# Smaller blocks in the recurrent stage of a hybrid decoder layer: 64-row diagonal blocks, 32x32 completions, alternating row halves, broadcasts by transposes

## The chip, the core and the metric

One of the cores of a Trainium2 chip runs the whole layer. The time is that of the device in microseconds (us), from one launch. TensorE is called PE here (its weight loads PEld), VectorE DVE, ScalarE ACT, GpSimd POOL, SyncE SP. All data are float32.

## The reference: what is computed

One decoder layer on 2048 tokens of width 1024. A root-mean-square norm and one input projection feed three branches, and one output projection adds them to the residual: differential attention (4 heads, two softmax maps each), a gated short convolution, and RWKV-7 time mixing. The change lies almost wholly in the last:

```
def step(state, inp):                  # per head, state is 64 x 64
    r_t, k_t, v_t, w_t, kk_t, a_t = inp
    sa = einsum('bhvk,bhk->bhv', state, kk_t)
    state = state * w_t - sa * (kk_t * a_t) + v_t * k_t
    y = einsum('bhvk,bhk->bhv', state, r_t)
```

It has 4 heads of 64. The output goes through a group norm per head and a gate.

## The kernel before

**Stages.** The kernel runs normalization and the first projections, then the recurrence of the first 1024 tokens (`rwkv(0)`), the attention of these tokens, the recurrence of the other 1024, their attention, and the output projection. Beside the recurrences and the attentions runs a *filler* stream: the remaining input projections (L343: 24 matmuls of 128x128 by 128x512 for one result) and at the end the output projection (L1194).

**The recurrence.** The steps are solved in chunks of 64 tokens. A *unit* is 256 tokens (4 chunks) of two heads, one head on partitions 0 to 63, the other on 64 to 127; a half has 8 units, the kernel 16. A unit goes through:

- `early`: decays, scaled keys, norms. The reciprocal norm of a token is broadcast over partitions by a matmul with the identity (`bc`, L538).
- `scores`: the products `G` of keys and queries inside the chunks (L572): per head 4 matmuls that contract over the 64 rows of that head, with 128 weight columns and 128 moving columns. DVE masks them into `N`, `BB` and `DE`. `N` is held as 128x128 matrices, of which only the two 64x64 diagonal blocks are not zero. The 32x32 diagonal blocks of `N` go through memory into another layout, `U`.
- `inverse`: DVE solves the 32x32 triangles (L638 to L649), and the inverses go through memory into the diagonal 32x32 blocks of `Z` (L653, L658).
- `late`: completes the 64x64 inverses. `Z` is transposed by PE (`xp`, L673, four 128x128), copied out by ACT, multiplied by `N` (`p4`, L680), masked and copied by ACT (L682), multiplied by `Z` (`p5`, L685), and added into `Z` by DVE (L688). Then `wu` (L696) applies the inverse, `mr` (L717, L718, 16 matmuls for each parity `e` of a chunk) makes the transition matrices `M` and `RW`, and four steps carry the state through the chunks: `chp` (L738), a copy of the state by DVE (L740), `yp` (L743). Group norm and gate follow, with a broadcast by matmul (`bcp`, L765).

**Order of the work.** PE runs strictly in the order in which the program issues its matmuls. The generators of the recurrence and the attention give a hint at every `yield` (in us); `run` multiplies it by a factor (0.6 and 0.55 for the two recurrences) and issues that much filler from the stream before it goes on. Between two pieces of `late(n)` lies one piece of the unit two ahead (`chain(n+2)`: `early`, `scores`, `inverse`). The order on the other engines is set by a planner when the program is built; each engine then runs its queue in order. DMAs are issued by SP. `ps_s` has three PSUM banks, which `xp`, `wu`, `mr`, `G` and `tp` take in turn; `ps_j` has two for the filler.

Outside the recurrence, `spread` (L251) broadcasts the input norm and `finish` in the attention (L1060) the norm of the result, both by matmuls with the identity. `hs`, `sr`, `nr` in the code are slices of 64 partitions.

Of the kernel before, what the change touches and what calls it, by code (L numbers as in the profile page):

```python
# [87 lines left out]
def _table(cols):  # L88
    t, o = {}, 0
    for n, w in cols:  # L90
# [7 lines left out]
                      ("eye", 32 * GW), ("hmean", 2), ("id64", 64), ("mB", 2)))  # L98
# [4 lines left out]
def host_consts():  # L103
# [21 lines left out]
    q = p % 64  # L125
    put("mB", np.stack([q >= 32, q < 32], 1))
# [19 lines left out]
def trunk(ctx, tc, a, o, phases="RTO"):  # L146
# [65 lines left out]
    # row blocks of the gated mix, transposed: heads by 256 tokens, conv and rwkv by 512  # L212
# [35 lines left out]
    def spread(rs, ps=None):  # L248
        ps = pj("hbc") if ps is None else ps
        for j in range(4):  # L250
            mm(ps[:, j * P:(j + 1) * P], rs[:, j:j + 1].broadcast_to([P, P]), ident, start=True, stop=True)  # L251
        bc = ap.tile([P, CK], F32, name="ccs", bufs=2)
        cpy(bc, ps)
        return bc
# [11 lines left out]
    def stats0(c, xs, pool, raw):  # L266
        """1/rms of the tokens, broadcast; with raw, the products with the unscaled input come first."""
# [40 lines left out]
    # ------------------------------------------------------------------ input projection  # L308
# [145 lines left out]
    # ------------------------------------------------------------------ rwkv  # L454
    def rwkv(half, pool):
# [15 lines left out]
        for i in range(2):  # L471
            m = {}
            for n, w in (("N", P), ("Z", P)):
                m[n] = pool.tile([P, NQ, w], F32, name=f"{n}{i}")
                nc.gpsimd.memset(m[n], 0.0)
            mats.append(m)
        P1 = pool.tile([P, NQ, P], F32, name="P1")
        nc.gpsimd.memset(P1, 0.0)
        mB = C("mB")
# [7 lines left out]
        def early(s, n, g, ct):  # L487
# [49 lines left out]
            for j in range(NJ):  # L537
                mm(bcp[:, j * P:(j + 1) * P], rnb[:, 2 * j:2 * j + 2].rearrange("p a b -> p (a b)"), ident,  # L538
                   start=True, stop=True)
# [9 lines left out]
        def scores(s):  # L549
# [17 lines left out]
            for jj in range(NJ // 2):  # L567
                for h in range(2):
                    G = pS("G")
                    for q in range(4):  # L570
                        j, e = jj * 2 + q // 2, q % 2
                        mm(G[:, q * P:(q + 1) * P], KB[h * 64:h * 64 + 64, j, 2 * e:2 * e + 2],  # L572
                           RA[h * 64:h * 64 + 64, :, j, 1 - e], start=True, stop=True)
                    Gv = G.rearrange("p (j e m t) -> p j e m t", j=2, e=2, m=2)
                    q0 = h * NJ + jj * 2
                    for e in range(2):
# [3 lines left out]
                        tt(N[sr, q0:q0 + 2, sr], Gv[sr, :, e, 1], lt[sr], ALU.mult)  # L580
# [7 lines left out]
            for e in range(2):  # L588
                for b in range(2):
                    q0 = (e * 2 + b) * NQ  # L590
                    r0 = 64 - 64 * e + b * 32
                    dma(ud[q0:q0 + NQ].rearrange("q s t -> s q t"), N[r0:r0 + 32, :, r0:r0 + 32])
# [39 lines left out]
        def inverse(s):  # L632
            U, Z = s["U"], s["Z"]
            # inverses of the 32x32 diagonal blocks by forward substitution, GW columns of one block per partition;
            # the odd rows are first freed of the even rows before them, so that two rows go at a time
# [18 lines left out]
            for e in range(2):  # L654
                for b in range(2):
                    q0 = (e * 2 + b) * NQ
                    r0 = 64 - 64 * e + b * 32
                    dma(Z[r0:r0 + 32, :, r0:r0 + 32], zd[q0:q0 + NQ].rearrange("q c i -> c q i"))  # L658

        def late(s):  # L660
# [4 lines left out]
            Z2 = Z.rearrange("p q (b n) -> p q b n", b=2)  # L665
            Pb2 = P1.rearrange("p q (b n) -> p q b n", b=2)
# [3 lines left out]
            X = T("X", (P, NQ, 64))  # L670
            xp = pS("xp")
            for q in range(NQ):
                nc.tensor.transpose(xp[:, q * P:(q + 1) * P], Z[:, q], ident)  # L673
            yield LQ[0]
            cpy(X.rearrange("p q (b n) -> p (q b) n", b=2), xp.rearrange("p (q n) -> p q n", n=64)[:, :, 0:32])
            yield LQ[0]
            p45 = pw("p45")
            p4, p5 = p45[:, 0:NQ * 64], p45[:, NQ * 64:2 * NQ * 64]
            for q in range(NQ):
                mm(p4[:, q * 64:(q + 1) * 64], N[:, q], X[:, q], start=True, stop=True)  # L680
            yield LQ[0]
            act(Pb2[:, :, :, 0:32], p4.rearrange("p (q b n) -> p q b n", q=NQ, b=2), AF.Copy, scale=mB[:, 0:1])  # L682
            yield LQ[0]
            for q in range(NQ):
                mm(p5[:, q * 64:(q + 1) * 64], P1[:, q], Z2[:, q, :, 32:64], start=True, stop=True)  # L685
            yield LQ[0]
            Z64 = Z.rearrange("p q (b n) -> p (q b) n", b=2)
            stt(Z64[:, :, 32:64], p5.rearrange("p (q n) -> p q n", n=32), mB[:, 1:2], Z64[:, :, 32:64], ALU.mult,  # L688
                ALU.add)
            yield LQ[0]  # L690
            # [W | U0]
            W = T("W", (P, NQ, 64))
            wu = pS("wu")
            for h in range(2):
                for j in range(NJ):
                    mm(wu[:, (h * NJ + j) * P:(h * NJ + j + 1) * P], Z[:, h * NJ + j], AB[:, j, h], start=True, stop=True)  # L696
# [6 lines left out]
            for r0 in (0, 64):  # L703
                nc.gpsimd.memset(Z[r0:r0 + 32, :, r0 + 32:r0 + 64], 0.0)
            dP4 = dP.rearrange("p (j e) n -> p j e n", e=2)
            yield LQ[1]
            # transition matrices and the read-out of the incoming state
# [671 lines left out]
```

## Time and profile before

| | us |
|---|---|
| median of 3 runs | 1854.19 |
| lowest, highest | 1853.9, 1865.09 |
| span of the profiled execution | 1855.8 |

| engine | busy us | share of the span |
|---|---|---|
| PE | 1723.0 | 93% |
| PEld | 1288.3 | 69% |
| DVE | 1228.7 | 66% |
| POOL | 817.9 | 44% |
| ACT | 737.5 | 40% |

The span is the profiled execution's own time, and durations come from it; it lies 0.1% above the median of the runs. Busy time is the union of an engine's instructions. A matmul's own duration holds its way through the array, so that the time one takes from the engine is read from start to start. A float32 matmul stands in the trace as two records, a transpose as one.

### The profile page before, as it was taken

The page shows a single profiled execution, that of the slowest core. Times are in us where ns is not written, and L with a number is a line of the kernel's source. Part 1 is how long each engine was busy: PE and PEld are TensorE (multiplying, and loading weights), DVE is VectorE, ACT ScalarE, POOL GpSimd, SP SyncE. Part 2 cuts the span into 40 slices and gives each one's busy share as a digit, 9 for nine tenths or more (in the row PEclk, how much of TensorE's full clock was granted, in tenths as well). Part 3 has the DMA queues.
Part 4 walks back from the last instruction along what each step waited for, and adds up shares of the span by engine and source line. Part 5 has one row for each costly group of instructions (what it writes and reads, how often), then busy time and mean ns, then how long its engine had stood idle before and what let it go on. Part 6 is the DMA issues. An engine that isn't in the chain of part 4 may idle for free.

```text
span 1855.8 us, 27286 instructions
## 1 busy us (share of the span) xinstructions
PE 1723.0 (93%) x9416; PEld 1288.3 (69%) x9416; DVE 1228.7 (66%) x2653; ACT 737.5 (40%) x1797; POOL 817.9 (44%) x786
## 2 busy tenths in 40 slices
PE   5899799999999889999799999999999989999998
PEld 4687576777776666777666767766666666767686
DVE  7534866656527888756766576357788888777742
ACT  5331111221126555532122221145565656666642
POOL 6443332333286776334222233473485473453233
PEclk8899898998999999999799998999999989999999
DMA  5342121222156442124222222351142243232223
GB/s 181 114 146 93 47 63 59 86 76 67 61 181 196 148 140 82 64 68 148 63 82 68 86 76 62 100 154 60 63 147 64 74 150 101 71 95 70 81 78 116
DMA packets 136586, 180.13 MB, mean 97 GB/s; under 512 B 34912, under 2 KB 83072, under 8 KB 136448
## 3 DMA queue, kind: packets, MB, share of 16 engines
q1 hardware_dynamic: 136448, 178.39, 30.8%
q8 instruction: 74, 1.21, 0.3%
q14 instruction: 64, 0.52, 0.1%
HBM read 132.18 MB, written 46.14 MB: 96 GB/s over the span
## 4 chain that ended last, share of the span: by engine, by line
PE 62%; DVE 25%; DMA 4%; issue 3%; SPq 2%; ACT 2%; POOL 1%; DVEq 0%; POOLq 0%; ACTq 0%
PE pj L343 27%; PE ops L1194 9%; PE S L938 6%; DVE tmpx L646 5%; PE aT L1021 3%; PE S L937 3%; DVE Xs L649 3%; PE G L572 2%; PE av L1012 2%; DVE P L986 2%; SPq L594 2%; PE av L1014 2%; PE av L1013 2%; DVE x L242 1%; DVE nm L943 1%
## 5 line engine op out<-in xcount | busy, mean ns | idle before, releaser
L343 PE MATMUL pj<-hh,wh 128*128 128x512 f32 x1008 | 424.4, 421 | 4.2 <-DVE raw L394 3.4
L343 PE MATMUL pj<-hl,wh 128*128 128x512 f32 x1008 | 423.8, 420 | 0.0
L343 PE MATMUL pj<-hh,wl 128*128 128x512 f32 x1008 | 423.2, 420 | 0.0
L946 ACT ACTIVATE P<-S,nm 128x512 f32<-128x512 f32 (+3 forms) x320 | 199.3, 623 | 162.9 <-DVE nm L943 143.6
L943 DVE TENSOR_REDUCE nm<-S 128x1 f32<-128x512 f32 (+3 forms) x320 | 192.5, 606 | 77.4 <-PE S L938 74.1
L329 POOL TENSOR_TENSOR wl<-wr,wh 128x1024 fp32r<-128x1024 f32 x85 | 209.6, 2465 | 46.8 <-ACT wh L324 41.2
L343 PEld LDWEIGHTS pj<-hh,wh 128*128 128x128 f32 x1008 | 195.9, 194 | 49.1 <-issue 7.6
L343 PEld LDWEIGHTS pj<-hl,wh 128*128 128x128 f32 x1008 | 195.7, 194 | 45.2 <-issue 9.7
L343 PEld LDWEIGHTS pj<-hh,wl 128*128 128x128 f32 x1008 | 195.4, 194 | 45.0 <-issue 7.9
L938 PE MATMUL S<-K,QL 64*128 64x512 f32 (+2 forms) x320 | 150.1, 469 | 0.0
L326 POOL TENSOR_SCALAR wh<-wr 128x1024 fp32r<-128x1024 f32 x70 | 76.5, 1093 | 162.5 <-PE pj L343 152.6
L986 DVE SCALAR_TENSOR_TENSOR P<-P,sc 128x512 f32<-128x512 f32 (+3 forms) x160 | 141.5, 910 | 4.5 <-ACT P L970 2.9
L646 DVE TENSOR_TENSOR tmpx<-U,Xs 128x16 f32<-128x16 f32 (+15 forms) x256 | 128.6, 502 | 6.6 <-POOL U L640 1.2
L938 PEld LDWEIGHTS S<-K,QL 64*128 64x128 f32 x320 | 58.8, 184 | 101.6 <-issue 99.4
L937 PE MATMUL S<-K,QH 128*128 128x512 f32 (+2 forms) x320 | 120.8, 378 | 8.0 <-ACT P L946 8.0
L1028 DVE TENSOR_TENSOR aTl<-aT,aTh 128x512 fp32r<-128x512 f32 x144 | 98.4, 686 | 35.2 <-ACT aTh L1027 34.4
L1027 ACT CAST aTh<-aT 128x512 fp32r<-128x512 f32 x144 | 83.7, 585 | 87.9 <-PE aT L1021 87.1
L942 DVE TENSOR_TENSOR S<-S,bt 128x256 f32<-128x256 f32 (+1 forms) x152 | 57.4, 379 | 90.6 <-PE S L938 86.6
L1021 PE MATMUL aT<-con,P 128*128 128x128 f32 x576 | 93.9, 289 | 22.4 <-DVE aTl L1028 17.4
L1194 PE MATMUL ops<-woh,wl 128*128 128x512 f32 x256 | 103.9, 406 | 0.0
L1194 PE MATMUL ops<-woh,wh 128*128 128x512 f32 x256 | 103.5, 404 | 0.0
L1194 PE MATMUL ops<-wol,wh 128*128 128x512 f32 x256 | 103.5, 404 | 0.0
(336 smaller groups left out, 3354.2 us busy)
## 6 DMA issues: line engine op xcount, KB each, us to landing
wr<-in_wt_dram SPq DMA_DIRECT2D x85, 512.0 KB, 3.7
rawk<-pk SPq DMA_DIRECT2D x96, 128.0 KB, 2.8
U<-ud SPq DMA_DIRECT2D x128, 64.0 KB, 2.2
rawq<-pq SPq DMA_DIRECT2D x128, 64.0 KB, 2.3
wr<-mx SPq DMA_DIRECT2D x128, 64.0 KB, 1.9
oxt<-in_x_dram SPq DMA_DIRECT2D x32, 256.0 KB, 3.2
out_dram<-oxt SPq DMA_DIRECT2D x32, 256.0 KB, 2.1
prw<-s SPq DMA_DIRECT2D x28, 256.0 KB, 2.1
```

Of the source, the lines that this page charges most:

```text
L329: nc.gpsimd.tensor_tensor(wl[:, ks], wr[:, ks], wh[:, ks].bitcast(F32), ALU.subtract)
L343: mm(ps, lhs[:, k], rhs[c][k], start=(n == 0), stop=(n == 3 * NK - 1))
L646: tt(tmp[:, :, :, 0:m], U[:, 0:m, i:i + 2].rearrange("p j r -> p r j").unsqueeze(2).broadcast_to([P, 2, GW, m]), Xs[:, 0:m].rearrange("p j ...
L937: mm(s[:, 0:sw], QH[:, m, off:off + P], K[:, m, 0:sw], start=True, stop=False)
L938: mm(s[:, 0:sw], QL[ms, off:off + P], K[ms, m, 0:sw], start=False, stop=True)
L943: nc.vector.tensor_reduce(nm[:, m, g:g + 1], s[:, 0:gw], AX.X, ALU.max, negate=True)
L946: act(p[:, 0:gw], s[:, 0:gw], AF.Exp, bias=nm[:, m, g:g + 1], accum_out=l[:, m, g:g + 1])
L986: stt(p1, p1, sc[:, 1, g:g + 1], p0, ALU.mult, ALU.add)
L1021: nc.tensor.transpose(t[:, d * 256 + qi * P:d * 256 + qi * P + P], x["A"][g][:, ko:ko + P], ident)
L1027: cpy(th, t)
L1028: tt(tl, t, th.bitcast(F32), ALU.subtract)
L1194: mm(ps, l[:, k], Ws[n][r][k], start=(c == 0), stop=(c == 3 * NK - 1))
```

## The change

- `N` and `Z` keep 64 columns instead of 128: of each 128x128 matrix only its two diagonal 64x64 blocks. `P1` shrinks to 32 columns and the mask `mB` goes.
- In `late` the transposes `xp` and their copy go: DVE transposes the 32x32 blocks (`nc.vector.transpose`). `p4` and `p5` become 8 matmuls each with 32 contracted rows, 32 weight columns and 32 moving columns, in turn in the upper and the lower 64 partitions; each result is copied in two pieces, one by ACT, one by DVE. There is one `yield LQ[0]` less.
- `wu` becomes 8 matmuls of 64x64 weights by 128 columns, in turn on the two halves of rows and columns. The two clearings of `Z` by POOL go.
- `mr`: both parities are issued as one group, row halves in turn, into two banks; their two `yield LQ[1]` become one of twice the size.
- `G`: the matmuls of the two heads are issued in turn, into two banks, ahead of any masking.
- The broadcasts `bc`, `bcp`, `hbc` (L251) and `obc` (L1060) become transposes instead of matmuls with the identity.

```diff
 def spread(rs, ps=None):
-            mm(ps[:, j * P:(j + 1) * P], rs[:, j:j + 1].broadcast_to([P, P]), ident, start=True, stop=True)
+            nc.tensor.transpose(ps[:, j * P:(j + 1) * P], rs[:, j:j + 1].broadcast_to([P, P]), ident)
...
 def rwkv(half, pool):
-            for n, w in (("N", P), ("Z", P)):
-                m[n] = pool.tile([P, NQ, w], F32, name=f"{n}{i}")
-                nc.gpsimd.memset(m[n], 0.0)
+            for n in ("N", "Z"):
+                m[n] = pool.tile([P, NQ, 64], F32, name=f"{n}{i}")
+            nc.gpsimd.memset(m["Z"], 0.0)
             mats.append(m)
-        P1 = pool.tile([P, NQ, P], F32, name="P1")
-        nc.gpsimd.memset(P1, 0.0)
-        mB = C("mB")
...
             for jj in range(NJ // 2):
+                Gs = [pS("G") for _ in range(2)]
+                for q in range(4):
+                    j, e = jj * 2 + q // 2, q % 2
+                    for h in range(2):
+                        mm(Gs[h][:, q * P:(q + 1) * P], KB[h * 64:h * 64 + 64, j, 2 * e:2 * e + 2],
+                           RA[h * 64:h * 64 + 64, :, j, 1 - e], start=True, stop=True)
                 for h in range(2):
-                    G = pS("G")
-                    for q in range(4):
-                        j, e = jj * 2 + q // 2, q % 2
-                        mm(G[:, q * P:(q + 1) * P], KB[h * 64:h * 64 + 64, j, 2 * e:2 * e + 2],
-                           RA[h * 64:h * 64 + 64, :, j, 1 - e], start=True, stop=True)
+                    G = Gs[h]
...
-                        tt(N[sr, q0:q0 + 2, sr], Gv[sr, :, e, 1], lt[sr], ALU.mult)
+                        tt(N[sr, q0:q0 + 2], Gv[sr, :, e, 1], lt[sr], ALU.mult)
...
-                    dma(Z[r0:r0 + 32, :, r0:r0 + 32], zd[q0:q0 + NQ].rearrange("q c i -> c q i"))
+                    dma(Z[r0:r0 + 32, :, b * 32:b * 32 + 32], zd[q0:q0 + NQ].rearrange("q c i -> c q i"))
...
 def late(s):
-            X = T("X", (P, NQ, 64))
-            xp = pS("xp")
-            for q in range(NQ):
-                nc.tensor.transpose(xp[:, q * P:(q + 1) * P], Z[:, q], ident)
-            yield LQ[0]
-            cpy(X.rearrange("p q (b n) -> p (q b) n", b=2), xp.rearrange("p (q n) -> p q n", n=64)[:, :, 0:32])
-            yield LQ[0]
+            X = T("X", (P, NQ, 32))
+            nc.vector.transpose(X, Z[:, :, 0:32])
+            P1 = T("P1", (P, NQ, 32))
             p45 = pw("p45")
-            p4, p5 = p45[:, 0:NQ * 64], p45[:, NQ * 64:2 * NQ * 64]
-            for q in range(NQ):
-                mm(p4[:, q * 64:(q + 1) * 64], N[:, q], X[:, q], start=True, stop=True)
-            yield LQ[0]
-            act(Pb2[:, :, :, 0:32], p4.rearrange("p (q b n) -> p q b n", q=NQ, b=2), AF.Copy, scale=mB[:, 0:1])
+            p4, p5 = p45[:, 0:NQ * 32], p45[:, NQ * 32:2 * NQ * 32]
             yield LQ[0]
             for q in range(NQ):
-                mm(p5[:, q * 64:(q + 1) * 64], P1[:, q], Z2[:, q, :, 32:64], start=True, stop=True)
+                for r0 in (0, 64):
+                    up, lo = slice(r0, r0 + 32), slice(r0 + 32, r0 + 64)
+                    mm(p4[lo, q * 32:(q + 1) * 32], N[up, q, 32:64], X[up, q], start=True, stop=True)
             yield LQ[0]
-            stt(Z64[:, :, 32:64], p5.rearrange("p (q n) -> p q n", n=32), mB[:, 1:2], Z64[:, :, 32:64], ALU.mult,
-                ALU.add)
+            cpy(P1[32:64], p4[32:64].rearrange("p (q n) -> p q n", n=32))
+            nc.vector.tensor_copy(P1[96:128], p4[96:128].rearrange("p (q n) -> p q n", n=32))
             yield LQ[0]
+            for q in range(NQ):
+                for r0 in (0, 64):
+                    up, lo = slice(r0, r0 + 32), slice(r0 + 32, r0 + 64)
+                    mm(p5[up, q * 32:(q + 1) * 32], P1[lo, q], Z[lo, q, 32:64], start=True, stop=True)
+            yield LQ[0]
+            cpy(Z[0:32, :, 32:64], p5[0:32].rearrange("p (q n) -> p q n", n=32))
+            nc.vector.tensor_copy(Z[64:96, :, 32:64], p5[64:96].rearrange("p (q n) -> p q n", n=32))
+            yield LQ[0]
...
-                    mm(wu[:, (h * NJ + j) * P:(h * NJ + j + 1) * P], Z[:, h * NJ + j], AB[:, j, h], start=True, stop=True)
+                    for hs in (slice(0, 64), slice(64, 128)):
+                        mm(wu[hs, (h * NJ + j) * P:(h * NJ + j + 1) * P], Z[hs, h * NJ + j], AB[hs, j, h], start=True,
+                           stop=True)
...
-            for r0 in (0, 64):
-                nc.gpsimd.memset(Z[r0:r0 + 32, :, r0 + 32:r0 + 64], 0.0)
...
+            mrs = [pS("mr")[:, 0:2 * WR // 2] for _ in range(2)]
+            for j in range(NJ):
+                for what in range(2):
+                    for h in range(2):
+                        hs, q = slice(h * 64, h * 64 + 64), h * NJ + j
+                        for e in range(2):
+                            sr = slice(64 - 64 * e, 128 - 64 * e)
+                            mm(mrs[e][hs, (what * NJ + j) * 64:(what * NJ + j) * 64 + 64], W[sr, q],
+                               DE[sr, q, e] if what else KBm[sr, j * 2 + e, hs], start=True, stop=True)
+            yield 2 * LQ[1]
             for e in range(2):
-                sr = slice(64 - 64 * e, 128 - 64 * e)
-                mr = pS("mr")[:, 0:2 * WR // 2]
-                for h in range(2):
-                    hs = slice(h * 64, h * 64 + 64)
-                    for j in range(NJ):
-                        q = h * NJ + j
-                        mm(mr[hs, j * 64:j * 64 + 64], W[sr, q], KBm[sr, j * 2 + e, hs], start=True, stop=True)
-                        mm(mr[hs, (NJ + j) * 64:(NJ + j) * 64 + 64], W[sr, q], DE[sr, q, e], start=True, stop=True)
-                yield LQ[1]
-                mr4 = mr.rearrange("p (m j n) -> p m j n", m=2, j=NJ)
+                mr4 = mrs[e].rearrange("p (m j n) -> p m j n", m=2, j=NJ)
```

The load of the 32x32 blocks of `N` into `ud` takes the new columns in the same way as that of `Z`. `bc` (L538), `bcp` (L765) and `obc` (L1060) change as `spread` does.

## Rows read from the trace of the kernel before

**Rows 1.** The page: span, busy time of each engine.
```profile
span 1855.8 us, 27286 instructions
PE 1723.0 (93%) x9416; PEld 1288.3 (69%) x9416; DVE 1228.7 (66%) x2653; ACT 737.5 (40%) x1797; POOL 817.9 (44%) x786
```

**Rows 2.** By stretch: us; busy us of PE, PEld, DVE, ACT, POOL; clock, DMA share, GB/s.
```profile
155.00:541.00 386.00, 358.92 (x2381) 278.44 (x2380) 236.19 (x619) 73.25 (x183) 135.13 (x144) 0.93 0.26 77
846.00:1219.00 373.00, 341.22 (x2317) 263.93 (x2316) 223.92 (x602) 75.51 (x184) 123.60 (x136) 0.94 0.29 85
281.00:293.00 12.00, 11.87 (x49) 8.52 (x48) 5.08 (x17) 2.26 (x7) 0.00 (x0) 0.50 0.13 29
```

**Rows 3.** PE in order of time, p5 among filler: start us, us, engine line, op, operands.
```profile
265.49 0.40 PE L343 MATMUL pj<-hh,wl 128*128 128x512 f32 x1
265.73 1.00 PE L685 MATMUL p<-Z,P 128*128 128x64 f32 x8
266.54 0.48 PE L343 MATMUL pj<-hh,wh 128*128 128x512 f32 x1
```

**Rows 4.** The same view: wu; then one half of mr among filler.
```profile
270.06 1.05 PE L696 MATMUL wu<-AB,Z 128*128 128x128 f32 x8
...
271.65 0.40 PE L343 MATMUL pj<-hh,wl 128*128 128x512 f32 x1
271.98 0.33 PE L717 MATMUL mr<-KBm,W 64*64 64x64 f32 x2
...
272.87 0.51 PE L343 MATMUL pj<-hh,wh 128*128 128x512 f32 x1
```

**Rows 5.** The same view: one head's scores G at full clock, between two filler matmuls.
```profile
237.82 0.49 PE L343 MATMUL pj<-hh,wl 128*128 128x512 f32 x1
238.25 1.16 PE L572 MATMUL G<-RA,KB 64*128 64x128 f32 x8
239.33 0.50 PE L343 MATMUL pj<-hh,wh 128*128 128x512 f32 x1
```

**Rows 6.** The same view: the recurrence's wait, then G at half clock.
```profile
280.39 0.48 PE L738 MATMUL chp<-Ss,M 64*64 64x64 f32 x4 [2.83 <-DVE Ss L740]
...
281.73 2.07 PE L572 MATMUL G<-RA,KB 64*128 64x128 f32 x8
```

**Rows 7.** PE in time: bvp, whose row and column halves alternate; then broadcast bcp.
```profile
247.95 0.40 PE L343 MATMUL pj<-hl,wh 128*128 128x512 f32 x1
248.28 0.68 PE L618 MATMUL bvp<-VU,BB 64*64 64x64 f32 x16
248.89 0.50 PE L343 MATMUL pj<-hh,wl 128*128 128x512 f32 x1
249.23 0.40 PE L343 MATMUL pj<-hh,wh 128*128 128x512 f32 x1
...
251.30 0.61 PE L765 MATMUL bcp<-con,sqy 128*128 128x128 f32 x4
```

**Rows 8.** The same view: lw and la, the two row halves with all 128 columns.
```profile
219.25 0.48 PE L496 MATMUL lw<-in_thw,wup 64*128 64x256 f32 x1
219.26 0.48 PE L498 MATMUL la<-in_thw,wup 64*128 64x256 f32 x1
```

**Rows 9.** The same view: the four transposes xp.
```profile
301.19 0.60 PE L673 MATMUL xp<-con,Z 128*128 128x128 f32 x4
301.54 0.48 PE L343 MATMUL pj<-hl,wh 128*128 128x512 f32 x1
```

**Rows 10.** SyncE's queue: the four loads of Z that those transposes read.
```profile
288.65 1.81 SPq L658 DMA_DIRECT2D Z<-zd  x4
```

**Rows 11.** What PE waited for in the whole span: total us, times, longest us.
```profile
PE chp L738 <- DVE Ss L740: 13.9, 10, 2.8
PE xp L673 <- DMA Z<-zd: 15.7, 3, 8.0
```

**Rows 12.** VectorE in the first recurrent stretch: the sum that completes Z; busy us, mean ns.
```profile
L688 DVE SCALAR_TENSOR_TENSOR Z<-p,conr,Z 128x256 f32<-128x256 f32 x8 | 3.8, 480 | 4.7 <-PE p L685 4.7
```

More of the change, by code (lines that the diff above doesn't have):

```diff
@@ L97 @@
 CONR, NCONR = _table((("le", 64), ("lt", 64), ("scan", WR), ("hones", 2), ("bones", 128), ("cmat", 128),
-                      ("eye", 32 * GW), ("hmean", 2), ("id64", 64), ("mB", 2)))
+                      ("eye", 32 * GW), ("hmean", 2), ("id64", 64)))
 T_Q, T_K, T_V, T_ZA, T_CB, T_CC, T_CH, T_ZC, T_RW, T_ZR = 0, 4, 8, 12, 16, 18, 20, 22, 24, 31
@@ L124, in host_consts @@
     put("id64", (p[:, None] % 64) == t[None])
-    q = p % 64
-    put("mB", np.stack([q >= 32, q < 32], 1))
     put("ones", np.ones((P, 1)))
@@ L537, in early @@
             for j in range(NJ):
-                mm(bcp[:, j * P:(j + 1) * P], rnb[:, 2 * j:2 * j + 2].rearrange("p a b -> p (a b)"), ident,
-                   start=True, stop=True)
+                nc.tensor.transpose(bcp[:, j * P:(j + 1) * P], rnb[:, 2 * j:2 * j + 2].rearrange("p a b -> p (a b)"),
+                                    ident)
             mm(bop, rko[:, ct], rk, start=True, stop=True)
@@ L591, in scores @@
                     r0 = 64 - 64 * e + b * 32
-                    dma(ud[q0:q0 + NQ].rearrange("q s t -> s q t"), N[r0:r0 + 32, :, r0:r0 + 32])
+                    dma(ud[q0:q0 + NQ].rearrange("q s t -> s q t"), N[r0:r0 + 32, :, b * 32:b * 32 + 32])
             for cg in range(NG):
@@ L664, in late @@
             dma(z, need(f"zr{ct}", gc)[:, o0:o0 + WR])
-            Z2 = Z.rearrange("p q (b n) -> p q b n", b=2)
-            Pb2 = P1.rearrange("p q (b n) -> p q b n", b=2)
             dP = T("dP", (P, NC, 64))
@@ L669, in late @@
                                     s["PC"].unsqueeze(2).broadcast_to([P, NC, 64]), ALU.mult)
-            X = T("X", (P, NQ, 64))
-            xp = pS("xp")
-            for q in range(NQ):
-                nc.tensor.transpose(xp[:, q * P:(q + 1) * P], Z[:, q], ident)
-            yield LQ[0]
-            cpy(X.rearrange("p q (b n) -> p (q b) n", b=2), xp.rearrange("p (q n) -> p q n", n=64)[:, :, 0:32])
-            yield LQ[0]
-            p45 = pw("p45")
-            p4, p5 = p45[:, 0:NQ * 64], p45[:, NQ * 64:2 * NQ * 64]
-            for q in range(NQ):
-                mm(p4[:, q * 64:(q + 1) * 64], N[:, q], X[:, q], start=True, stop=True)
-            yield LQ[0]
-            act(Pb2[:, :, :, 0:32], p4.rearrange("p (q b n) -> p q b n", q=NQ, b=2), AF.Copy, scale=mB[:, 0:1])
+            X = T("X", (P, NQ, 32))
+            nc.vector.transpose(X, Z[:, :, 0:32])
+            P1 = T("P1", (P, NQ, 32))
+            p45 = pw("p45")
+            p4, p5 = p45[:, 0:NQ * 32], p45[:, NQ * 32:2 * NQ * 32]
             yield LQ[0]
             for q in range(NQ):
-                mm(p5[:, q * 64:(q + 1) * 64], P1[:, q], Z2[:, q, :, 32:64], start=True, stop=True)
+                for r0 in (0, 64):
+                    up, lo = slice(r0, r0 + 32), slice(r0 + 32, r0 + 64)
+                    mm(p4[lo, q * 32:(q + 1) * 32], N[up, q, 32:64], X[up, q], start=True, stop=True)
             yield LQ[0]
-            Z64 = Z.rearrange("p q (b n) -> p (q b) n", b=2)
-            stt(Z64[:, :, 32:64], p5.rearrange("p (q n) -> p q n", n=32), mB[:, 1:2], Z64[:, :, 32:64], ALU.mult,
-                ALU.add)
+            cpy(P1[32:64], p4[32:64].rearrange("p (q n) -> p q n", n=32))
[8 more added lines that the diff above has]
+            nc.vector.tensor_copy(Z[64:96, :, 32:64], p5[64:96].rearrange("p (q n) -> p q n", n=32))
             yield LQ[0]
@@ L764, in late @@
             for j in range(NJ):
-                mm(bcp[:, j * P:(j + 1) * P], rvb[:, 2 * j:2 * j + 2].rearrange("p a b -> p (a b)"), ident,
-                   start=True, stop=True)
+                nc.tensor.transpose(bcp[:, j * P:(j + 1) * P], rvb[:, 2 * j:2 * j + 2].rearrange("p a b -> p (a b)"),
+                                    ident)
             yield LQ[1]
@@ L1059, in finish @@
             for j in range(2):
-                mm(bc[:, j * P:(j + 1) * P], rp[:, j:j + 1].broadcast_to([P, P]), ident, start=True, stop=True)
+                nc.tensor.transpose(bc[:, j * P:(j + 1) * P], rp[:, j:j + 1].broadcast_to([P, P]), ident)
             stt(ob, ob, DV(15), bc[:, 0:256], ALU.mult, ALU.mult)
```

## The prediction

> **What bounds the kernel now.** I read the page first: PE is busy 1723.0 of 1855.8 us, every other engine far less [rows 1]. The table by stretches says whether that holds where the change lies. In the two recurrent stretches, 386 and 373 us, PE is busy 359 and 341 (93% and 91%), DVE only 236 and 224 (61% and 60%), and the granted clock is 0.93 and 0.94 [rows 2]. Outside them PE is busy for the other 1023 of 1097 us. So PE's queue sets the pace everywhere, and an edit is worth what it takes out of that queue, unless PE then stands in a wait that it had not reached before. The list of PE's waits shows where that can be: on the copy of the state, 13.9 us in 10 waits, and on the loads of Z, 15.7 us in 3 [rows 11]. At 280 us PE waits 2.83 us for such a copy, and from 281 to 293 the granted clock is 0.50, the 1.2 GHz level: a group of eight G records then keeps PE busy 2.07 us, not 1.16 [rows 2, 5, 6].
>
> **How a group is priced.** Filler surrounds the small groups, so I take the time from the last filler start before a group to the first one after, less the 0.24 us that a filler matmul holds PE (265.49 to 265.73) [rows 3]. p5: 1.05 - 0.24 = 0.81. One half of mr: 1.22 - 0.24 = 0.98 [rows 4]. G of one head: 1.51 - 0.24 = 1.27 [rows 5]. bvp: 0.94 - 0.24 = 0.70 [rows 7]. After a group the first filler takes 0.34 and not 0.24 (248.89 to 249.23) [rows 7]: a group that goes or is merged saves 0.10 more.
>
> **The change, per unit (16 units).**
>
> *xp goes*: 301.19 to 301.54 is 0.35 [rows 9], and 0.10 for the return: **-0.45**. The wait for Z that stood before it moves to DVE's transpose (below).
>
> *p4, p5*: each 8 full-size records before, 16 small ones after, upper and lower partitions in turn. No row has 32x32 weights. The nearest is bvp: 16 records, halves in turn on both sides of the array, 0.70. Below: half the columns, so half its time, 0.35. Above: mr's half, whose halves come four matmuls at a time, 0.98. I take 0.70: 2 x 0.11 = **-0.22** (ends -0.92 and +0.34).
>
> *wu*: its eight records take 0.81 as those of p5 do (270.06 on; 1.05 us busy against 1.00) [rows 3, 4]. After it are 16, of 64x64 weights by 128 columns. A G record, also 128 columns, costs 1.08/8 = 0.135, one of bvp 0.61/16 = 0.038, so 0.076 for a pair [rows 5, 7]. Eight pairs at the longer stream: 0.70 + 8 x 0.059 = 1.17; G's own group, 1.27, is the same stream. I take 1.2: **+0.40**. Below +0.36; above, no overlap, 16 x 0.135 = 2.16: +1.35.
>
> *mr*: 1.96 for two groups. After, one group of 32 records. At bvp's rate, the entry of 0.09 (0.33 against 0.24) paid once: 2 x 0.70 - 0.09 = 1.31. If all four 64x64 corners run at once, 0.70; if no more overlaps than now, 1.96. bvp has the same tile and columns, so I take 1.31: -0.65, and 0.10 for the return: **-0.75** (ends -1.36 and -0.10).
>
> *G*: 2 x 1.27 before. lw and la, the two row halves under all 128 columns into two banks, start at 219.25 and 219.26 [rows 8]: such halves do run side by side. G's heads now alternate like that, so one group of 1.27 and one return less: **-1.37**. Without overlap, -0.10.
>
> *bc, bcp*: two matmuls with the identity are four records [rows 7]; four transposes are four records in 0.35, 0.09 each [rows 9]. Two records less in each: 4 x 0.09 = **-0.36**. That transposes of a broadcast read are slower no row shows; at twice the time the gain is nothing.
>
> Sum -0.45 - 0.22 + 0.40 - 0.75 - 1.37 - 0.36 = **-2.75 us**, 44 us for 16 units, and 47 at the granted 0.93 to 0.94. Outside the recurrence hbc loses 16 records and obc 64, at 0.09: 7 us. PE's queue gets 54 us shorter.
>
> *What costs nothing, and its cover.* One yield of 0.9 goes per unit, times 0.6 or 0.55: about 8 us of filler run later, where PE sets the pace as well. On DVE the completion of Z, 0.48 [rows 12], becomes a transpose of 128 columns and two copies; between 0.2 and 0.48 each that is +0.1 to +1.0 per unit on an engine that is 40% idle here. I take +0.5. If that cover is gone, it is 8 us. ACT trades two copies for two smaller ones. POOL loses two clearings that waited for wu. No DMA is added or moved: SP's queue is as before. Both banks of G and of mr are held at once, of three; the copies out of wu stand before them in the chain anyway.
>
> *The added wait*: DVE's transpose waits for the loads of Z. Behind it in DVE's queue stand the state copies that PE waits for and the evacuation of the filler, which has two banks. Today the four loads start at 288.65 and take 1.81 to issue, and xp reads at 301.19 [rows 9, 10]: some 10 us of slack. A unit gets 3 us shorter, so most of it stays. Late next are the state copies.
>
> *What is given back.* In the 3 units where PE already waits for the loads [rows 11], a shorter queue only lengthens the wait: 3 x 2.75 = 8. Shorter mr and G put PE sooner at the state copies; I let each of the 10 waits grow by 0.5: 5 us (nothing at best, 14 if they double). Net 54 - 13 = 41: the profiled 1855.8 becomes 1815, and as its span lies 1.6 above the median of the runs, **1813**.
>
> **One rule against it.** bvp's two row halves write one bank, and its 16 records take 0.70, where mr's 16 of the same shape, which change row halves only between its two groups, take 0.98 [rows 4, 7]. The Trainium skill, "TensorEngine Tiling (Array Packing)", "Restrictions and Gotchas", says that different row tiles cannot access the same PSUM bank at once. By that rule wu, p4 and p5, each in one bank, would gain no overlap, and the forecast would be that of rival 2; the bvp row speaks against it where the halves write different partitions, as all three do.
>
> **Rivals.**
> 1. *More overlap*: mr at 0.70 and p4, p5 at 0.35 each. For it: lw and la start 0.01 apart [rows 8]. Against: no row has four corners at work. 1.31 more per unit, 22 us: 1791. Chance 0.12.
> 2. *Halves in one bank take turns*: p4, p5 at 0.98, wu at 2.16: 0.56 + 0.96 = 1.52 more per unit, 26 us: 1839. Chance 0.07.
> 3. *The recurrence becomes the bound*: PE reaches copies and loads sooner than DVE and DMA deliver. For it: rows 11, and the half clock that follows such a wait [rows 6]. Against: DVE at 61%. If two thirds of the units' 47 us turn into waits: 54 - 31 = 23, so about 1831 to 1838. Chance 0.13.
> 4. *Slower: the DVE transpose stands in front.* If the planner puts it right behind the end of the inverse in DVE's queue, DVE stands still while the loads of Z issue and land, with the copies and the filler's evacuation behind it. No gain from a stall of 54/16 = 3.4 us per unit on; at 6 us it is 96 - 54 = +42: 1896. For it: the order on DVE is planned, and it does wait in line for other engines. Against: the 10 us of slack. Chance 0.05.
>
> **How the numbers follow.** The forecast has the other 0.63: 1813, its own range 1798 to 1830. The bounds worked through: best (rival 1 with nothing given back) 1780; worst with the overlap of G kept, p4, p5 and wu at their upper ends and mr at 1.31, 1845. The range 1788 to 1843 holds the forecast, rivals 2 and 3 and most of rival 1. About 1% (18.5 us) is what a measurement of this kernel can tell from no change. Faster than 1835.6: forecast 0.62, rival 1 0.12, half of rival 3: 0.81. Within: rival 2, the rest of 3, some of 4 and the forecast's tail: 0.15. Slower: 0.04.
>
> **What would show it.** Right: a mr group of 32 records near 1.3, one G group of 16 near 1.3 at full clock, p4 and p5 near 0.7, wu near 1.2, two-record broadcasts near 0.2; the recurrent stretches about 20 us shorter each; PE's waits for Z and for the state copies up by under 15 us. Wrong: G records that do not pair, wu near 2, DVE idle on the loads of Z at its transpose, or granted clock below 0.90 in these stretches.

## The result and the profile after

| | before | changed |
|---|---|---|
| median of 6 runs | 1854.05 | 1871.87 |
| lowest, highest | 1848.75, 1865.09 | 1865.17, 1875.09 |
| span of the profiled execution | 1855.8 | 1872.3 |

The ratio is 1.0084, 95% interval 1.0058 to 1.011: the change makes the kernel 0.8% slower, where 2.2% faster (1813) was forecast. The page of the changed kernel answers to [rows 1]:

```profile
span 1872.3 us, 27635 instructions
PE 1684.0 (90%) x9592; PEld 1224.4 (65%) x9592; DVE 1243.8 (66%) x2685; ACT 734.6 (39%) x1797; POOL 803.3 (43%) x748
```

PE is busy 39 us less and the span is 16.5 us longer. PE's groups in order of time, as in [rows 3 to 5] (start us, us):

```profile
306.06 0.40 PE L341 MATMUL pj<-hh,wh 128*128 128x512 f32 x1
306.38 0.44 PE L683 MATMUL p<-Z,P 32*32 32x32 f32 x16
306.75 0.50 PE L341 MATMUL pj<-hl,wh 128*128 128x512 f32 x1
...
310.58 0.39 PE L341 MATMUL pj<-hh,wh 128*128 128x512 f32 x1
310.90 1.09 PE L694 MATMUL wu<-AB,Z 64*64 64x128 f32 x16
311.92 0.50 PE L341 MATMUL pj<-hl,wh 128*128 128x512 f32 x1
...
314.59 0.40 PE L341 MATMUL pj<-hh,wh 128*128 128x512 f32 x1
314.92 0.34 PE L714 MATMUL mr<-KBm,W 64*64 64x64 f32 x8
...
315.54 0.50 PE L341 MATMUL pj<-hl,wh 128*128 128x512 f32 x1
...
238.50 0.51 PE L341 MATMUL pj<-hh,wl 128*128 128x512 f32 x1
238.94 1.16 PE L567 MATMUL G<-RA,KB 64*128 64x128 f32 x16
240.03 0.50 PE L341 MATMUL pj<-hh,wh 128*128 128x512 f32 x1
```

Priced as before (filler start to filler start less 0.24): p5 0.45 (p4 0.46 in the same way), wu 1.10, all of mr 0.71, G of both heads 1.29. G's 16 records stand in the same 1.16 us as 8 did [rows 5]. Every group is within 0.02 us of the forecast or cheaper. So look at the stages. Busy time of PE, PEld, DVE, ACT, POOL, then clock, DMA share and GB/s, cut at the same events in both kernels (first `lw` of a recurrence, first score of an attention); first before, then changed:

```profile
155.50:541.30 385.80, 358.72 (x2380) 278.52 (x2380) 236.19 (x619) 73.25 (x183) 135.43 (x144) 0.93 0.26 77
541.30:845.80 304.50, 284.80 (x1356) 208.56 (x1354) 221.11 (x480) 161.69 (x434) 181.61 (x188) 0.98 0.39 123
845.80:1219.30 373.50, 341.72 (x2319) 264.34 (x2319) 223.94 (x602) 75.71 (x185) 124.10 (x136) 0.94 0.29 85
1219.30:1855.80 636.50, 609.24 (x2847) 434.90 (x2845) 468.59 (x876) 364.28 (x874) 303.25 (x267) 0.98 0.30 93
```

```profile
157.30:542.40 385.10, 334.51 (x2484) 245.05 (x2484) 246.91 (x635) 70.05 (x181) 126.37 (x126) 0.91 0.26 75
542.40:861.00 318.60, 286.26 (x1318) 207.61 (x1316) 222.94 (x480) 163.18 (x434) 179.45 (x185) 0.95 0.37 117
861.00:1227.50 366.50, 319.05 (x2420) 233.36 (x2421) 232.39 (x618) 73.95 (x183) 114.21 (x116) 0.90 0.28 85
1227.50:1872.30 644.80, 615.45 (x2861) 437.11 (x2859) 464.96 (x876) 365.06 (x877) 311.15 (x272) 0.98 0.30 94
```

Three things are to be seen. The recurrences lost 24 and 23 us of PE's work and got 0.7 and 7 us shorter: the rest is idle, 51 and 47 us after 27 and 32, and the granted clock fell from 0.93 and 0.94 to 0.91 and 0.90. The first attention holds the same work and takes 14.1 us more. The last stretch takes 8.3 us more, with more PE work in it. With 1.8 us ahead of the first recurrence that is the 16.5. Filler alone (us, then busy us of PE and PEld with their records) shows where that extra work comes from; before, then changed, first and second recurrence:

```profile
155.50:541.30 385.80, 252.19 (x852) 158.31 (x851) 0.93 0.26 77
845.80:1219.30 373.50, 234.24 (x782) 143.86 (x782) 0.94 0.29 85
```

```profile
157.30:542.40 385.10, 247.04 (x832) 157.47 (x831) 0.91 0.26 75
861.00:1227.50 366.50, 231.25 (x764) 145.03 (x764) 0.90 0.28 85
```

38 filler matmuls, at 0.235 us some 9 us, went from stretches in which PE now stands idle to the last one, where it hardly does. And PE's waits (total us, times, longest us), against [rows 11]:

```profile
PE chp L736 <- DVE Ss L738: 27.6, 24, 4.1
PE chp L736 <- DVE M L719: 16.5, 12, 3.5
...
PE p L675 <- DVE Xs L646: 11.4, 1, 11.4
```

### The profile page after: what moved, and what is told of

Read it like the earlier page. It is cut to its first block, busy times and chain, and to the rows that moved or that the text cites. A ratio compares the mean times of both kernels' runs of the same rounds, so it can differ in the third digit from the quotient of the medians.

```text
span 1872.3 us, 27635 instructions
## 1 busy us (share of the span) xinstructions
PE 1684.0 (90%) x9592; PEld 1224.4 (65%) x9592; DVE 1243.8 (66%) x2685; ACT 734.6 (39%) x1797; POOL 803.3 (43%) x748
## 3 DMA queue, kind: packets, MB, share of 16 engines
q8 instruction: 76, 1.25, 0.3%
## 4 chain that ended last, share of the span: by engine, by line
PE 56%; DVE 30%; DMA 4%; issue 3%; ACT 2%; SPq 2%; POOL 1%; DVEq 0%; POOLq 0%; ACTq 0%
PE pj L341 25%; PE ops L1192 9%; DVE tmpx L643 5%; PE S L936 5%; PE aT L1019 3%; DVE Xs L646 3%; PE S L935 3%; PE av L1010 2%; DVE P L984 2%; SPq L591 2%; PE av L1012 2%; PE av L1011 2%; DVE nm L941 1%; DVE x L240 1%; PE G L567 1%
## 5 line engine op out<-in xcount | busy, mean ns | idle before, releaser
L341 PE MATMUL pj<-hh,wh 128*128 128x512 f32 x1008 | 430.9, 427 | 7.6 <-DVE raw L392 5.3
L341 PE MATMUL pj<-hl,wh 128*128 128x512 f32 x1008 | 430.3, 427 | 0.0
L341 PE MATMUL pj<-hh,wl 128*128 128x512 f32 x1008 | 427.7, 424 | 0.0
L341 PEld LDWEIGHTS pj<-hh,wl 128*128 128x128 f32 x1008 | 199.8, 198 | 47.1 <-issue 9.9
L984 DVE SCALAR_TENSOR_TENSOR P<-P,sc 128x512 f32<-128x512 f32 (+3 forms) x160 | 136.8, 886 | 4.2 <-ACT P L968 2.3
L643 DVE TENSOR_TENSOR tmpx<-U,Xs 128x16 f32<-128x16 f32 (+15 forms) x256 | 121.4, 474 | 8.5 <-POOL U L637 3.0
```

The costliest lines, as they stand in the source:

```text
L341: mm(ps, lhs[:, k], rhs[c][k], start=(n == 0), stop=(n == 3 * NK - 1))
L643: tt(tmp[:, :, :, 0:m], U[:, 0:m, i:i + 2].rearrange("p j r -> p r j").unsqueeze(2).broadcast_to([P, 2, GW, m]), Xs[:, 0:m].rearrange("p j ...
L984: stt(p1, p1, sc[:, 1, g:g + 1], p0, ALU.mult, ALU.add)
```

## The experiments

Each ratio is to the kernel before, with its 95% interval; that kernel was run again beside each group of experiments, at medians of 1855.9 to 1859.2 us. The theories: A, a loop through DVE and the trips of U sets the length of a unit; B, the change's own waits; C, the lost yield; D, the completion itself; E to G, what holds PE in the recurrences.

**More filler in the recurrences of the changed kernel.**

```diff
-SCALE = (0.6, 1.0, 0.55, 1.0)
+SCALE = (0.66, 1.0, 0.605, 1.0)
```

> The changed kernel with a tenth more filler issued inside the two recurrences (the factors 0.6 and 0.55 become 0.66 and 0.605: some 160 filler matmuls of 0.235 us, about 37 us, move from the later stages into them). Theory A (the loop): the length of a unit is set by a loop through DVE, PE (G), the two DMA trips of U and back to DVE, so PE stands idle in the recurrences and takes more filler for nothing: the recurrent stretches (385 and 366 us) grow by less than 12 us each, and the time falls from 1872 to about 1845. Theory B (the change's own waits: the order of PE's work has new waits that stretch with it): the stretches grow by the whole filler, 18 us each, and the time stays at 1872.

Measured: 1900.82 us, ratio 1.0244 (1.0203 to 1.0286). Both theories missed the total. The recurrences did take 135 more filler matmuls, 32 us, for 11 and 6 us more, half the price that B has. But the last stretch, with 142 filler matmuls fewer in it than in the changed kernel, got longer: 652 us with 51 us of PE idle, after 645 with 29. The second attention seems to need the filler as cover; no run here tried that by itself.

**Half of the inverse left out**, in the changed kernel and in the one before.

```diff
-            for i in range(0, 32, 2):
+            for i in range(0, 32, 4):
```

> The changed kernel with half of the 16 row pairs of the inverse left out (8 products and 8 sums less on DVE per unit, 0.47 + 0.31 us each, 6 us per unit). Theory A: the loop is 6 us shorter, and the PE time that the change saved can come out: stretches near 340 and 325, total near 1785, and at least 25 us below the kernel before with the same part left out. Theory B: it falls no more than the kernel before does with the same part left out; the gap of +16 us between the two stays.

> The kernel before with the same half of the inverse left out. Theory A: PE's queue and the loop were about equally long there, so PE soon sets the pace: the time falls by some 30 to 40 us, to about 1815, well short of the 96 us that left DVE. Theory B: as much as the changed kernel falls.

Measured: 1816.91 (0.9798, 0.977 to 0.9825) and 1815.94 (0.9788, 0.9755 to 0.982). The changed kernel falls by 55 us, the one before by 38: the gap closes, and doesn't turn to -25. A is refuted as the sole bound. From the start of a unit's inverse to the next it took 41.3 us on average (units 2 to 6 of each half, counted from 0), of these 23.1 in the inverse; with half of it 13.0, and the unit 38.7: of 10 us, 2.6 came out.

**Only the edits to G, mr and the broadcasts, on the kernel before.** The diff is that part of the change. It leaves the amount of filler alone, but not the number of yields: the two `yield LQ[1]` behind `mr` are one of twice the size here too.

> The kernel before with only the edits that save PE time and leave DVE, ACT, POOL and the number of yields alone: G and mr alternate row halves, the four broadcasts are transposes; N, Z, xp, p4, p5 and wu as before. By the measured groups this takes some 2.5 us per unit and 7 us outside from PE, 47 us in all. Theory A: the recurrent stretches keep their length within 8 us, PE waits longer in them, and the time is 1854 within 12 us. Theory B: the new waits lie in the completion of Z, which is as before here, so the time falls by 30 us or more, to about 1820.

Measured: 1837.81, ratio 0.9905 (0.987 to 0.994): 18 us faster, between the theories. In its profile PE's busy time falls by 26 and 23 us in the recurrences and these get 8.6 and 10.6 us shorter: 40% comes out. PE's waits in that kernel:

```profile
PE chp L741 <- DVE Ss L743: 24.6, 19, 2.8
PE xp L675 <- DMA Z<-zd: 15.0, 3, 7.9
PE chp L731 <- DVE VU L704: 10.7, 8, 2.4
```

So the remaining edits, the completion of Z with its one yield less, cost 34 us.

**Yields as before, and the filler alone as before.**

```diff
             p4, p5 = p45[:, 0:NQ * 32], p45[:, NQ * 32:2 * NQ * 32]
             yield LQ[0]
+            yield LQ[0]
...
-            yield 2 * LQ[1]
+            yield LQ[1]
+            yield LQ[1]
```

> The changed kernel with as many yields in late as before: one more LQ[0] ahead of p4, and the doubled LQ[1] after mr split in two. Filler in the recurrences goes back from 831 and 764 matmuls to 851 and 782, and the early pieces of the unit two ahead lie between the same pieces of late as before. Theory C (the lost yield): the 34 us by which the changed kernel is slower than the kernel before with only the edits to G, mr and the broadcasts (1838) are 38 filler matmuls run later (9 us), the making of the normalized second half falling at another place of the first attention (318.6 us there against 305.5: 13 us), and the closer packing (12 us): the first attention is back at 305 +- 3, the time near 1840. Theory D (the completion itself, DVE's transpose and small copies): the time stays above 1860.

```diff
             p4, p5 = p45[:, 0:NQ * 32], p45[:, NQ * 32:2 * NQ * 32]
-            yield LQ[0]
+            yield 2 * LQ[0]
```

> The changed kernel with the missing 0.9 us of filler put back by doubling the first LQ[0] of late, without another place for an early piece. Theory C: the first attention is back at 305 +- 3 and the end 9 us shorter, but the packing stays: near 1850. If the filler count alone matters, as low as with the yields back. Theory D: above 1860, the recurrent stretches longer by the 5 us of filler each.

Measured: 1840.40, ratio 0.991 (0.9879 to 0.994), and 1852.00, 0.9963 (0.9931 to 0.9995). C is borne out, D is not: two yields, no computation, are worth 32 us, of which 20 come with the amount of filler. Which of the two places gives the other 12 was not separated. With the yields back:

```profile
154.00:537.80 383.80, 332.17 (x2509) 246.35 (x2508) 246.37 (x635) 71.02 (x183) 131.51 (x128) 0.92 0.26 77
537.80:844.40 306.60, 283.58 (x1316) 205.62 (x1314) 224.96 (x481) 161.49 (x435) 180.88 (x185) 0.97 0.40 123
844.40:1202.00 357.60, 311.06 (x2447) 230.86 (x2447) 230.35 (x618) 73.66 (x183) 119.99 (x121) 0.93 0.30 89
1202.00:1836.00 634.00, 607.19 (x2815) 431.11 (x2813) 462.52 (x876) 363.45 (x874) 300.86 (x266) 0.98 0.30 93
```

Against the changed kernel: first attention -12.0, second recurrence -8.9, last stretch -10.8, first recurrence -1.3, with 38 filler matmuls more in the recurrences. Another 3.3 us of the 36 between these two profiles lie ahead of the first recurrence, where the kernels are the same. PE's line of the page, to be held against that of the changed kernel, and then the second recurrence with the amount of filler alone put back:

```profile
PE 1661.1 (90%) x9592; PEld 1213.6 (66%) x9592; DVE 1242.0 (68%) x2685; ACT 732.1 (40%) x1797; POOL 805.1 (44%) x748
```

```profile
847.60:1217.70 370.10, 325.76 (x2446) 239.29 (x2447) 234.80 (x618) 73.52 (x183) 119.60 (x121) 0.89 0.29 86
```

The same 9592 records keep PE busy 1684.0 us in the changed kernel and 1661.1 here, at a granted clock of 0.938 and 0.948 over the span. So 23 of the 36 us are the same instructions taking longer, and 13 are idle time. In the second recurrence all of the loss is of that kind: PE is idle 47 us in the changed kernel, 46.5 with the yields back and 44 with the amount alone, and is busy 319, 311 and 326, at 0.90, 0.93 and 0.89 (the last two with the same filler).

**Two queues for the loads of U**, on top of the yields.

```diff
-                dma(U[cg:P:NG], ud)
+                (nc.scalar.dma_start if cg % 2 else dma)(U[cg:P:NG], ud)
```

> The changed kernel with the yields back, and four of the eight loads of U issued by ACT's queue instead of SP's. The eight issues take 0.59 us each in a row, so U arrives some 2.4 us earlier. Theory A (the length of a unit is set by the loop from U through the inverse, the scores, G, the masks and the two DMA trips back to U): the recurrent stretches shorten by 12 to 19 us each against the same kernel with one queue (8 x 2.4 = 19 at most). If PE's own queue sets the pace instead: within 5 us of it.

Measured: 1876.22 (1.0104, 1.0047 to 1.0162), 36 us slower than with one queue, so it tells nothing for A. ACT's four issues take 2.59 us in which its copies wait, and PE, which waited 1.4 us there in all, waits for one of them:

```profile
331.77 2.59 ACTq L591 DMA_DIRECT2D U<-ud  x4
...
PE vpp L754 <- ACT AB L610: 22.7, 12, 3.6
```

**The completion alone**: the changed kernel with G, mr and the broadcasts as before.

> The kernel before with only the completion of Z changed (64-column N and Z, DVE transpose, small p4, p5 and wu, one yield less); G, mr and the broadcasts as before. By the groups of the changed kernel PE saves 0.45 + 0.35 + 0.35 - 0.30 = 0.85 us per unit by it, 14 us. Theory C: slower than before all the same by 10 to 25 us, with the first attention near 318 and 38 filler matmuls later. Theory D: slower by the same, but with the loss in the recurrent stretches and the first attention near 305.

Measured: 1884.55 (1.0127, 1.0062 to 1.0192), +28.5 us, somewhat more than either theory had. The first attention takes 321 us and the last stretch 642 against 636, as C has it, but the first recurrence is also 9 us longer, with 20 filler matmuls fewer.

**One yield less on the kernel before, nothing else.**

```diff
                 nc.tensor.transpose(xp[:, q * P:(q + 1) * P], Z[:, q], ident)
-            yield LQ[0]
```

> The kernel before with nothing changed but one yield LQ[0] of late left out (the one behind xp). Theory C (the lost yield costs by itself): 38 filler matmuls run later, 9 us, the making of the normalized second half falls at another place of the first attention, 10 us or more there, and the early pieces lie one place closer: slower by 15 to 30 us, near 1877. If the yield is worth nothing, as the prediction had it: 1854 within 5.

Measured: 1890.78, ratio 1.0166 (1.0113 to 1.0219): 33 us slower, somewhat more than expected. This is as much as the whole turn of sign, on a kernel that has none of the change. Its four stages:

```profile
154.80:551.60 396.80, 362.02 (x2356) 279.69 (x2356) 242.29 (x619) 73.11 (x181) 129.34 (x141) 0.92 0.25 72
551.60:873.20 321.60, 291.05 (x1358) 214.00 (x1357) 223.19 (x480) 163.07 (x434) 182.33 (x189) 0.95 0.37 117
873.20:1237.10 363.90, 333.84 (x2292) 258.63 (x2293) 224.92 (x602) 76.71 (x183) 118.25 (x133) 0.95 0.29 86
1237.10:1884.00 646.90, 618.46 (x2893) 442.47 (x2892) 462.24 (x876) 363.08 (x877) 309.27 (x271) 0.98 0.31 93
```

Against the kernel before: +11.0, +17.1, -9.6 and +10.4. The first attention and the end lose as they do in the changed kernel. The recurrences do not: there the first kept its length and the second lost, here the first loses and the second gains. So the parts agree in two stages of four, and that the sums agree so well (33 and 32) is in part luck.

**20 filler matmuls between the first recurrence and the first attention** of the changed kernel.

```diff
         run(rwkv(0, bp), SCALE[0], "rwkv0")
+    for _ in range(20):
+        pull()
```

> The changed kernel with 20 filler matmuls issued in a row between the first recurrence and the first attention, so that the attention meets the filler stream at the place where the kernel before met it. Theory C: the attention, which took 318.6 us, falls to 305 + 4.7 for the 20 matmuls = 310, the end comes another 4.7 us earlier, the second recurrence keeps its loss: near 1859. If the place of the filler stream does not matter for the attention: 318 + 4.7 there and 1872.

Measured: 1874.57 (1.0082, 1.0058 to 1.0105). The attention itself does what C says, 306.4 us after 318.6:

```profile
549.00:855.40 306.40, 283.55 (x1314) 205.10 (x1312) 222.46 (x480) 160.94 (x434) 178.55 (x183) 0.97 0.39 122
```

The total misses: first recurrence and burst took 9.0 us more, the second recurrence 5.3, the end 2.7. So the place of the filler stream is worth 12 us to the attention, but moving it this way moves other things as well, and the kernel as a whole gained nothing. In the changed kernel's attention PE waits 8.94 us for a combined softmax row (`P`, L984) that stands in DVE's queue behind the scaling of the second half's input (`xk`, L240), which the filler stream brings along:

```profile
648.24 1.62 DVE L240 SCALAR_TENSOR_TENSOR xk<-xk,vec,ccs 128x512 f32<-128x512 f32 x1
...
649.85 3.57 DVE L240 SCALAR_TENSOR_TENSOR xk<-xk,vec,ccs 128x512 f32<-128x512 f32 x2
...
653.34 0.74 DVE L984 SCALAR_TENSOR_TENSOR P<-P,sc 128x512 f32<-128x512 f32 x1
...
654.13 0.90 PE L1019 MATMUL aT<-con,P 128*128 128x128 f32 x3 [8.94 <-DVE P L984]
```

PE's wait for `P` in the whole first attention, in the kernel before, in the changed one, in the one with the 20 matmuls ahead, and in the kernel before with one yield less:

```profile
PE aT L1021 <- DVE P L986: 1.0, 1, 1.0
PE aT L1019 <- DVE P L984: 11.5, 3, 8.9
PE aT L1019 <- DVE P L984: 1.6, 1, 1.6
PE aT L1020 <- DVE P L985: 12.0, 4, 8.9
```

The long wait is there in the two kernels in which the stream is 20 matmuls behind, and not in the two in which the attention meets it at its old place.

**Yields back and half of the inverse left out.**

> The changed kernel with the yields back and half of the 16 row pairs of the inverse left out. The kernel before with the same part left out took 1816. Theory E (in the recurrences PE waits on DVE; of what PE saves some 40% comes out): with DVE's work shorter PE has less to wait for, and the gap to the kernel before grows from -16 (1840 against 1856) to -25 or more: 1790 or less. If the wait has another source than DVE's queue: the gap stays at -16, 1800.

Measured: 1799.38 (0.9663, 0.9616 to 0.971): 16.6 us below the kernel before with the same half, as with the whole inverse (by the two ratios, each to its own runs beside it, 23 us). In the profiles the two recurrences are together 15 us shorter than those of the kernel before with the same half, after 18 with the whole inverse. E is not borne out: where it looked for the gain, a shorter inverse does not free what PE saved.

**Yields back, more filler in the second recurrence, less in the second attention**: `SCALE = (0.6, 1.0, 0.605, 0.93)`.

> The changed kernel with the yields back, a tenth more filler in the second recurrence (0.55 becomes 0.605) and 7% less in the second attention, so that the attention doesn't run out of filler as it did when only the recurrences took more. From the run with more filler in both recurrences: 65 to 78 matmuls more lengthened the second one by 6 us and are worth 15 to 18 us later: near 1830. If the attention starves all the same: 1840 or more.

Measured: 1852.32 (0.9975, 0.9943 to 1.0006), 12 us slower than without. The second recurrence grew by 13 us for 59 filler matmuls, 14 us, and nothing came back: filler is not free there once the yields are back.

**The copy of the state on ACT**, with the yields back and on the kernel before.

```diff
-                nc.vector.tensor_copy(sst[ct] if c == NC - 1 else Ss[:, c + 1], chp[:, c * 64:(c + 1) * 64])
+                cpy(sst[ct] if c == NC - 1 else Ss[:, c + 1], chp[:, c * 64:(c + 1) * 64])
```

> The changed kernel with the yields back and the copy of the state between the chunk steps moved from DVE to ACT. Theory F (the copy stands behind other work in DVE's queue; ACT is busy a fifth of the recurrences): PE's waits at chp, 20 us in the first recurrence, fall below 8, the recurrent stretches shorten by 8 us or more each, and the time is 1822 or less against 1840. Theory G (the wait is the way PE to copy to PE itself, or moves to the next place that DVE serves): the stretches stay within 5 us.

> The kernel before with the same move of the state copy. Its waits at chp are 13.9 us in both recurrences. Theory F: it gains less than the changed kernel, at most 10 us, about 1847. Theory G: within 5 us of 1856.

Measured: 1819.38, ratio 0.9798 (0.9757 to 0.9839), and 1844.27, 0.9908 (0.9871 to 0.9945). On either engine one copy takes 0.21 to 0.22 us; what it stood behind in DVE's queue made the wait. With the yields back, copy on DVE, then on ACT:

```profile
PE chp L738 <- DVE Ss L740: 31.0, 22, 3.8
PE chp L728 <- DVE VU L702: 18.9, 12, 2.7
```

```profile
PE chp L728 <- DVE VU L702: 13.1, 8, 3.1
PE chp L738 <- DVE M L721: 4.3, 5, 1.9
PE chp L738 <- ACT Ss L740: 0.7, 2, 0.5
```

31.0 us of waits become 0.7. About half of them only moved: PE's idle time in the two recurrences falls by 16 us. The recurrences get 15.7 and 2.4 us shorter, and the gap between the two kernels grows from 16 to 25 us, a step that is hardly larger than the intervals. F holds for the first recurrence and the sum; the second got less than the 8 us expected. The kernel before gained 15 us on its runs of the same group, more than the 10 that F allowed it. The changed kernel with the yields back and the copy on ACT is faster than the kernel before and the changed one.

**The same filler, more of it before the chunk steps**: `LQ = (0.6, 0.65, 0.835, 3.0, 2.0)` instead of `(0.9, 0.5, 0.385, 3.0, 2.0)`, with the yields back.

> The changed kernel with the yields back and the same filler per unit placed otherwise: the hints LQ 0.9, 0.5, 0.385 become 0.6, 0.65, 0.835, so that 0.27 us more filler lies before each chunk step and less between the pieces of the completion. If the waits at chp are only uncovered, they fall by half and the stretches shorten by 5 us or more each: 1830 or less. If the pieces of the completion need their cover as much, waits appear at p5 and wu instead: 1840 or more.

Measured: 1837.02 (0.9894, 0.9854 to 0.9933), the same as without within the intervals. PE's waits for the copy are 30.8 us, as with the yields back alone (31.0), so they did not fall by half: more filler ahead of the chunk steps does not cover them, and it is no way to a gain.

## Why the prediction was wrong

The forecast of 1813 is missed by 59 us. Some 32 of them belong to the yields, which were put at nothing, and the other 27 to PE's saved time, most of which did not come out. The time lies outside the range.

- *PE's groups*: right in kind, and worth more than said. mr was put at 1.31 and measured 0.71: its four corners do run at once, which rival 1 had. p4 and p5 were put at 0.70 and p5 measured 0.45; wu 1.2 and 1.10; G 1.27 and 1.29. The broadcasts were put at 0.36 for the two; `bcp` alone falls from 0.44 to 0.21 and `bc` by as much, 0.45. Summed as in the prediction, a unit gives PE 4.0 us instead of 2.75: 0.45 + 2 x 0.35 - 0.29 + 1.25 + 0.10 + 1.25 + 0.10 + 0.45.
- *The rule on banks*, which the prediction quotes from the Trainium skill, "TensorEngine Tiling (Array Packing)", "Restrictions and Gotchas": the trace of the changed kernel disagrees with it for halves that write different partitions. wu, in one bank, takes 1.10, where without overlap it was put at 2.16. Rival 2 falls.
- *"PE's queue sets the pace everywhere"* failed first. Outside the recurrences no run tested it by itself, and the 12 us of the first attention speak against it. Inside, 93% busy did not mean that an edit is worth what it takes out of the queue. With the edits to G, mr and the broadcasts alone, 40% came out; with everything and the yields back, PE is busy 57 us less in the two recurrences and these are 18 us shorter. The rest became waits: PE's idle time there grew by 39 us, where 13 us were put down as given back. DVE, put at 0.5 us more per unit on a cover of 40% idle time, is busy 19 us more in the two recurrences of the changed kernel, 1.2 per unit. Over the span, with the yields back, PE's wait for the copy of the state grew from 13.9 to 31.0 us, that for the copies out of wu (`VU`) from 4.4 to 18.9. Rival 3 had this mechanism and 1831 to 1838; with the yields back it is 1840. That the copy's wait comes from its place in DVE's queue was shown by moving it. What holds the rest, on the copies out of wu for instance, was not tried. The completion of `Z`, 0.9 us per unit of PE's saving, added nothing: with the edits to G, mr and the broadcasts alone the kernel takes 1838, with everything and the yields back 1840.
- *"One yield of 0.9 goes, it costs nothing"* failed worst and turned the sign. I counted its filler as work that costs the same later, and did not count the place of the second yield, behind mr, at all. The first left out alone costs the kernel before 33 us; both put back give the changed kernel 32. Measured parts, by stages with the yields back: 12 us in the first attention, where the filler stream meets DVE at another place; 11 us at the end, 9 of them the 38 filler matmuls; 9 us in the second recurrence. That the attention's part comes from the place of the stream is shown. The second recurrence loses by the granted clock and not by longer waits (0.90 against 0.93, PE as idle as before); what lowers the clock there was not tried, and in the kernel before, with the yield left out, that recurrence did not lose.
- *The granted clock* was taken from the kernel before, 0.93 to 0.94. It came out at 0.91 and 0.90 in the recurrences, at the edge of what the prediction named as a sign of being wrong, and the same PE records took 23 us longer than with the yields back. These 23 us are part of the 32 above, not a further loss.
- *The DVE transpose in front* (rival 4): it takes 0.31 us and waits 15.1 us in all, in 8 of 16 units, for the loads of Z. No run moved it; PE's idle time just ahead of p4 is 18.6 us, where it waited 15.7 ahead of xp. With the yields back the same transposes stand in a kernel that is faster than before, so rival 4 does not decide.
- *The bounds of the range*: 1780 and 1845 do not come out of their terms as given, which make 1778 (1791 less the 13 us given back) and 1839 (1813 and the 26 us of rival 2). The measured time lies outside either way.

So the change in its arithmetic is worth 16 us here, and the two hints that went with it cost 32.

## What to carry to other kernels

In a schedule written by hand a yield is a part of the work's order: keep the number and the amount of hints when groups are removed, or price their loss by leaving one out of the kernel before, alone. A busy share of 93% in a stretch does not say that the engine's queue is the bound: look up, for each shortened group, what it produces, in whose queue the consumer stands, and what is ahead of it there. When saved time does not come out, move the smallest instruction that the engine waits for to an idle queue before touching the large work. Keep idle time apart from the time that the same instructions take: here the second was 23 of the 36 us between two profiles.

## What the runs showed of the hardware

- Four 64x64 corners with float32 operands work at once: mr's 32 records hold PE for 0.71 us among filler, where two groups of 16, the halves four matmuls apart, took 1.96 [rows 4].
- Two row halves under all 128 columns do the same: G's 16 records stand in the 1.16 us of 8 [rows 5].
- A broadcast by transpose needs half the records of one by a float32 matmul with the identity (`bcp` x2, not x4 [rows 7]).
- DMAs issued from ACT hold up ACT's own work: four issues took 2.59 us there.
- The granted clock is part of what a wait costs: the same 9592 PE records took 1684.0 us at 0.938 over the span, 1661.1 at 0.948 and, with the copy of the state on ACT as well, 1652.5 at 0.954.
